# First relative bias formed behind the first slice, its tables loaded ahead of the second projection, and the front's loads put in another order

## The chip, the cores and the metric

One core of a Trainium2 chip runs the program. The metric is the device time of one execution in microseconds (us). Three runs of the kernel before took 691.38, 693.18 and 688.67 us: median 691.38.

## The reference, cut to what matters

Two layers of a decoder trunk, 256 tokens of width 1024. The change lies in the first half of layer 0, the "even mixer".

```python
cond = silu(c)
mod = cond @ ada_w[0] + ada_b[0]            # six vectors of 1024: shift, scale, gate (mixer), shift, scale, gate (ffn)
h = rmsnorm(x, mix_pre_g[0]) * (1 + scale_m) + shift_m
proj = h @ w_in                             # 1024 x 3072: qa, ka, va, qb, kb, vb, 512 columns each
# 8 heads in group a, 8 in group b, 64 wide; every head:
logit = q k^T / 8 + rel_bias[head, bucket(t - s)]      # causal
o = softmax(logit) v
y = concat(o_a, o_b) @ w_out
x = x + gate_m * rmsnorm(y, mix_post_g[0])
# then a gated feed-forward with a causal convolution of width 3, and layer 1
```

With 256 tokens group a's single block and group b's first window both become dense causal softmax attention with a bias that depends on the distance of two tokens alone; the kernel adds what the further windows of group b weigh through a table (k_reach).

## The kernel before, in words

Products of f32 are made of three matmuls each (mm3): a weight is split by ScalarE into a rounded upper part (..h, L315) and by VectorE into the remainder (..l, L316); the activations are likewise hh and hl. Engines: TensorE (PE) multiplies, VectorE (DVE) and ScalarE (ACT) split, form h, and do the softmax; SyncE (SP) issues the weight loads.

Order of work. On PE, DVE and ACT a scheduler chooses the order from the program's dependencies. SP's order is the program's own up to `in_order.close()`, and from there the scheduler places SP's DMAs too. SP has eight semaphores for its DMAs, so each waits for the one eight before it; a DMA into a buffer also waits until the buffer is free. Tiles of tag aw (a quarter of an ada_w slab, `first_ws`) have four buffers, raw weights four.

The front:
- x and c are loaded; `ada_first_load` (from L240) brings the columns of ada_w for two k-tiles as four tiles (aw_first), two DMAs each; vec_a holds ada_b and the norms' gains, turned to vT by one transposition.
- `ada_first(i)` (L220 to L238) forms shift and scale for the two k-tiles of slice i: 16 matmuls with the weights moving (`ada_main`, L154), a copy to part (L228), four transpositions (L232), three small DVE steps (L235 to L238). For slice 0, idle matmuls (`keep_clock`) stand before it and between copy and transpositions.
- `SLICES` cuts the 1024 rows of w_in into four slices of two k-tiles. Slice i loads rawaqk (two DMAs, L794) and rawav (L308), then the next slice's aw_first; turns x (xTm, L358); forms hh (L367), hsm on ACT (L371) and hl (L373); calls `ada_first(i + 1)`; and multiplies psa_q, psa_k (L813) and psa_v (L323 to L325), which add up over the slices.

Behind the fourth slice the relative bias is formed: rel_bias transposed (ps_rb, L825), multiplied with a one-hot matrix (ps_bias, L829), k_reach added (L830), and written to DRAM 32 times over (bias_d, L832, 16 x 32 x 384 f32, 786 KB). The loads of conv vectors (vec_b, L845 to L848) follow. `bias_tables` (from L854) then reads bias_d back, shifted by one element per row, into bt tiles: eight DMAs of 131 KB for the eight heads of a group. `attend` adds bt to the scores while it takes the row maximum (ltab, L582), exponentiates, transposes and multiplies with v. `qkv_proj` forms psb (L477) and psb_v for group b from rawb and rawbv; `out_proj` forms y0m (L692). `more_ada` spreads further columns of ada_w (aw_2048 and on, L143) over these parts; one kind sums on DVE (acc, L199), another on PE (L154).

## Time and profile before

| what | us |
|---|---|
| median of three runs | 691.38 |
| their range | 688.67 to 693.18 |
| the profiled execution | 693.11 |
| its span (first to last instruction) | 690.4 |
| busy: PE / DVE / ACT | 668.0 / 525.3 / 369.7 |
| mean granted clock of TensorE | 0.993 |

The profile is of one execution, 1.73 us above the median, with 2.71 us outside its span. PE's busy time is modelled for pipelined matmuls, so a busy PE is not PE at its peak: the issue cadence of matmuls (0.12 us for 256 columns, 0.23 us for 512) says what the work itself needs. A number in square brackets behind a timeline's row is the idle time before it and what ended it.

### The profile page before, as it was taken

Reading aid. Unit: us, or ns where it says so; the run is one execution under the profiler, and the core shown is the slowest. Engines: PE = TensorE matmul, PEld = TensorE weight load, DVE = VectorE, ACT = ScalarE, POOL = GpSimd, SP = SyncE. Lnnn points to the kernel's source line nnn. Section 1 sums busy time; section 2 is a strip of 40 time slices with the busy share of each in tenths; the row PEclk is TensorE's granted clock in tenths of the full one; section 3 lists DMA queues with packets and bytes.
Section 4 is the critical chain, followed back from the end, with each engine's and each line's share of the span. In section 5 each row is a group of like instructions: output and inputs, shape, how many; then the busy total and the mean of one; then the engine's idle time right before and its main releaser. Section 6 shows DMA issues by size and latency. Waiting matters only on the chain.

```text
span 690.4 us, 11784 instructions
## 1 busy us (share of the span) xinstructions
PE 668.0 (97%) x4547; PEld 574.7 (83%) x4547; DVE 525.3 (76%) x1008; ACT 369.7 (54%) x645; POOL 32.8 (5%) x95
## 2 busy tenths in 40 slices
PE   7889999999999999999999999999999999999996
PEld 5777976476899999999986998767599999999995
DVE  1454558688899999999978787774788777777785
ACT  3433455655565555555655645864565555555552
POOL 2000000001000000000001002410200000000000
PEclk9899999999999999999999999999999999999999
DMA  7799998996858878888875867622267555555611
GB/s 249 261 321 388 294 290 287 299 373 237 293 191 299 268 257 302 264 257 277 281 275 184 289 219 272 212 75 92 80 188 231 193 183 183 183 184 186 188 53 61
DMA packets 100819, 159.11 MB, mean 230 GB/s; under 512 B 4088, under 2 KB 62612, under 8 KB 100764
## 3 DMA queue, kind: packets, MB, share of 16 engines
q1 hardware_dynamic: 100739, 158.35, 68.9%
q8 instruction: 35, 0.57, 0.3%
q14 instruction: 21, 0.16, 0.1%
q10 hardware_dynamic: 24, 0.02, 0.0%
HBM read 156.52 MB, written 1.84 MB: 229 GB/s over the span
## 4 chain that ended last, share of the span: by engine, by line
PE 82%; DMA 7%; DVE 4%; ACT 2%; issue 1%; POOL 1%; SPq 1%; DVEq 0%; POOLq 0%; ACTq 0%
PE u L477 36%; PE y1f L692 9%; PE y0f L692 9%; PE psd L477 3%; DMA aw_first<-in_ada_w 3%; PE y1m L692 2%; DMA bias_d<-bias 2%; PE y0m L692 2%; DMA aw<-in_ada_w 1%; DMA bt<-bias_d 1%; PE ada L154 1%; PE psa_q L813 1%; PE psa_k L813 1%; PE ada_first L154 1%; ACT junknm L335 1%
## 5 line engine op out<-in xcount | busy, mean ns | idle before, releaser
L741 ACT ACTIVATE cv<-u,cvT 128x256 f32<-128x256 f32 x88 | 49.2, 561 | 65.6 <-PE u L477 61.7
L477 PE MATMUL u<-hh,wu_0h 128*128 128x256 f32 x352 | 69.9, 280 | 1.2 <-DVE hh L431 1.2
L477 PE MATMUL u<-hh,wu_1h 128*128 128x256 f32 x352 | 70.1, 280 | 0.0
L477 PE MATMUL u<-hh,wu_1l 128*128 128x256 f32 x352 | 69.9, 279 | 0.0
L477 PE MATMUL u<-hh,wu_0l 128*128 128x256 f32 x352 | 69.5, 279 | 0.0
L315 ACT CAST wu_1h<-rawu 128x1024 fp32r<-128x1024 f32 x44 | 46.3, 1051 | 31.1 <-PE y1f L692 17.6
L742 DVE SCALAR_TENSOR_TENSOR cv<-u,cvT,cv 128x255 f32<-128x255 f32 x88 | 42.1, 478 | 26.9 <-ACT cv L741 26.8
L199 DVE SCALAR_TENSOR_TENSOR acc<-aw,cpad,acc 128x512 f32<-128x512 f32 x77 | 57.8, 751 | 0.9 <-DMA aw<-in_ada_w 0.4
L477 PEld LDWEIGHTS u<-hh,wu_0h 128*128 128x128 f32 x352 | 54.7, 188 | 4.2 <-PE ada L276 1.4
L316 DVE TENSOR_TENSOR wu_0l<-rawu,wu_0h 128x1024 fp32r<-128x1024 f32 x44 | 53.6, 1221 | 5.3 <-ACT wu_0h L315 5.3
L315 ACT CAST wu_0h<-rawu 128x1024 fp32r<-128x1024 f32 x44 | 46.0, 1046 | 18.9 <-PE u L477 18.9
L316 DVE TENSOR_TENSOR wu_1l<-rawu,wu_1h 128x1024 fp32r<-128x1024 f32 x44 | 53.6, 1219 | 3.0 <-ACT wu_1h L315 2.9
L477 PEld LDWEIGHTS u<-hh,wu_1l 128*128 128x128 f32 x352 | 53.7, 188 | 0.0
L477 PEld LDWEIGHTS u<-hh,wu_1h 128*128 128x128 f32 x352 | 53.7, 188 | 0.0
L477 PEld LDWEIGHTS u<-hh,wu_0l 128*128 128x128 f32 x352 | 53.5, 188 | 0.0
L477 PE MATMUL u<-hl,wu_1h 128*128 128x256 f32 x352 | 48.2, 279 | 0.0
L477 PE MATMUL u<-hl,wu_0h 128*128 128x256 f32 x352 | 48.2, 279 | 0.0
L315 ACT CAST wd_0h<-rawd 128x1024 fp32r<-128x1024 f32 x26 | 27.3, 1049 | 35.3 <-PE u L477 29.9
L477 PEld LDWEIGHTS u<-hl,wu_1h 128*128 128x128 f32 x352 | 44.2, 188 | 0.0
L477 PEld LDWEIGHTS u<-hl,wu_0h 128*128 128x128 f32 x352 | 44.2, 188 | 0.0
L744 DVE SCALAR_TENSOR_TENSOR cv<-u,cvT,cv 128x254 f32<-128x254 f32 x88 | 41.8, 478 | 1.4
L316 DVE TENSOR_TENSOR wd_0l<-rawd,wd_0h 128x1024 fp32r<-128x1024 f32 x26 | 31.8, 1222 | 13.6 <-ACT wd_0h L315 13.5
(556 smaller groups left out, 1561.3 us busy)
## 6 DMA issues: line engine op xcount, KB each, us to landing
rawu<-in_ffn_w_up SPq DMA_DIRECT2D x44, 1024.0 KB, 5.5
aw<-in_ada_w SPq DMA_DIRECT2D x80, 512.0 KB, 6.6
rawd<-in_ffn_w_down SPq DMA_DIRECT2D x22, 1024.0 KB, 4.9
aw_first<-in_ada_w SPq DMA_DIRECT2D x32, 256.0 KB, 5.9
rawaqk<-in_ab_w_in SPq DMA_DIRECT2D x8, 512.0 KB, 6.5
rawb<-in_ab_w_in SPq DMA_DIRECT2D x4, 1024.0 KB, 13.9
rawd<-in_cd_w_in SPq DMA_DIRECT2D x4, 1024.0 KB, 5.8
rawc<-in_cd_w_in SPq DMA_DIRECT2D x4, 544.0 KB
```

Of the source, the lines that this page charges most:

```text
L154: last_main[:] = [nc.tensor.matmul(ps[32 * j:32 * j + 32, 0:cols], cpad[:, k, :], ws[k // 2][:, k % 2, 0:cols], start=(n < 4), stop=(n >= ...
L199: nc.vector.scalar_tensor_tensor(acc, w, c_k, acc, op0=ALU.mult, op1=ALU.add)
L315: nc.scalar.copy(hi, src)
L316: low = nc.vector.tensor_tensor(lo, src, hi.bitcast(F32), op=ALU.subtract)
L335: nc.scalar.activation(junk, src, AF.Square, scale=D ** -0.5, accum_out=ss)
L477: nc.tensor.matmul(dst(f), w[:, k, f * P:(f + 1) * P], h[:, 4 * u + k, :], start=(u == 0 and first(f) and f not in seen), stop=(u == 1 and ...
L692: last_down[:] = [nc.tensor.matmul(ys[t][:, h, :], g[p // 2][:, t * P:(t + 1) * P], wu[p % 2][:, h * 512:(h + 1) * 512], start=start and p ...
L741: nc.scalar.activation(tt[:, s, :], u_ps, AF.Identity, bias=cvT[:, bcol:bcol + 1], scale=col(2))
L742: nc.vector.scalar_tensor_tensor(tt[:, s, 1:S], u_ps[:, 0:S - 1], col(1), tt[:, s, 1:S], op0=ALU.mult, op1=ALU.add)
L744: nc.vector.scalar_tensor_tensor(tt[:, s, 2:S], u_ps[:, 0:S - 2], col(0), tt[:, s, 2:S], op0=ALU.mult, op1=ALU.add)
L813: nc.tensor.matmul((pq, pk)[f // 4][:, f % 4 // 2, f % 2 * S:(f % 2 + 1) * S], w[:, f * P:(f + 1) * P], h[:, kk, :], start=(kk == 0 and f ...
```

## The change

- The first slice's aw_first loads stand in one run, ahead of vec_a; the three small loads for the bias move behind the second slice's aw_first.
- `ada_first` becomes a generator that pauses behind its copy, so that vT is turned behind slice 0's `ada_main`, not ahead of it. Slice 0's copy moves from ACT to DVE, and its idle matmuls between copy and transpositions go from six calls to three.
- The bias is formed behind slice 0's products; bias_d is written from slice 1's place in SP's order, ahead of rawaqk of slice 2.
- Group a's eight bt loads stand in slice 3's place, behind its rawav. So they are ahead of rawb, the weights of group b's projection.
- The conv vectors are loaded and turned behind that projection, in the part whose order the scheduler chooses; SP's fixed order now ends ahead of `attend`.

```diff
--- before.py
+++ after.py
@@ -107,8 +107,8 @@
 
     vec_c = const.tile([8, P], F32, name="vec_c")
     nc.sync.dma_start(vec_c, c.rearrange("b (k p) -> (b k) p", p=P))
-    def turned(src, n, name):
-        ps = bank(f"ps_{name}", "a")
+    def turned(src, n, name, tag="a"):
+        ps = bank(f"ps_{name}", tag)
         nc.tensor.transpose(ps[:, :n], src[:n, :], ident[:n, :n])
         dst = const.tile([P, n], F32, name=name)
         nc.vector.tensor_copy(dst, ps[:, :n])
@@ -225,9 +225,10 @@
             keep_clock(before)
         ps, part = bank(f"ada_first{i}", "a"), small(f"part_first{i}", tag="part")
         ada_main(ps, first_ws[i], cols, i > 0)
-        nc.scalar.copy(part[:, 0:cols], ps[:, 0:cols])
+        (nc.scalar.copy if i else nc.vector.tensor_copy)(part[:, 0:cols], ps[:, 0:cols])
         if behind:
             keep_clock(behind, last_main[0])
+        yield
         for b in range(2 * n):
             nc.tensor.transpose(ps[:, b * P:(b + 1) * P], part[:, b * P:(b + 1) * P], ident)
         k = slice(k0, k0 + n)
@@ -769,23 +770,28 @@
         xns.append(normed(t, ss, f"m0_{t}"))
     first_mods = const.tile([P, 2, KT], F32, name="first_mods")
     B, A = first_mods[:, 0, :], first_mods[:, 1, :]
-    first_ws = {0: [ada_first_load(0, u) for u in range(2)]}
+    first_ws = {0: [ada_first_load(0, u) for u in range(4)]}
     vec_a = small("vec_a", (P, P), tag="o")
     nc.sync.dma_start(vec_a[0:96, :], ada_b.rearrange("l (k p) -> (l k) p", p=P))
     nc.sync.dma_start(vec_a[96:112, :], mix_pre_g.rearrange("l (k p) -> (l k) p", p=P))
     nc.sync.dma_start(vec_a[112:128, :], ffn_pre_g.rearrange("l (k p) -> (l k) p", p=P))
-    rb = small("rb", (16, 32), tag="o")
-    oh = small("oh", (32, TW), tag="o")
-    bias = small("bias", (16, TW), tag="o")
-    for dst, src in ((rb, rel_bias), (oh, k_onehot), (bias, k_reach)):
-        nc.sync.dma_start(dst, src)
-    first_ws[0] += [ada_first_load(0, u) for u in range(2, 4)]
-    vT = turned(vec_a, P, "vT")
-    ada_first(0, 9, 6)
+    first = ada_first(0, 9, 3)
+    next(first)
+    vT = turned(vec_a, P, "vT", "g")
+    list(first)
     w_in = ab_w_in[0]
     qkv = qkv_tiles("a")
     pq, pk = y_tile("psa_q"), y_tile("psa_k")
     pv = [bank(f"psa_v{t}") for t in range(2)]
+    def bias_tables(h0):
+
+        t = qkv_tile(f"bt{h0}")
+        for i in range(4):
+            nc.sync.dma_start(t[32 * i:32 * i + 32], bass.AP(
+                tensor=bias_d.tensor, offset=bias_d.offset + h0 * 32 * TW + P - 1 - 32 * i,
+                ap=[[TW - 1, 32], [32 * TW, 4], [1, S]]))
+        return t
+
 
     for i, (k0, n) in enumerate(SLICES):
         w = w_in[k0 * P:(k0 + n) * P]
@@ -795,6 +801,17 @@
         raw_v = load(w[:, 1024:1536], n, 512, f"rawav_{i}")
         if i + 1 < len(SLICES):
             first_ws[i + 1] = [ada_first_load(i + 1, u) for u in range(4)]
+        if i == 0:
+            rb = small("rb", (16, 32), tag="o")
+            oh = small("oh", (32, TW), tag="o")
+            bias = small("bias", (16, TW), tag="o")
+            for dst, src in ((rb, rel_bias), (oh, k_onehot), (bias, k_reach)):
+                nc.sync.dma_start(dst, src)
+        if i == 1:
+            bias_d = dram.tile([16, 32, TW], F32, name="bias_d")
+            nc.sync.dma_start(bias_d, bias[:, None, :].to_broadcast([16, 32, TW]))
+        if i == 3:
+            tabs_a = [bias_tables(4 * g) for g in range(2)]
         xb = bank(f"xTm0_{i}")
         ks = list(range(k0, k0 + n))
         xT = {k: xb[:, (k - k0) * S:(k - k0 + 1) * S] for k in ks}
@@ -802,7 +819,7 @@
             turn(xT, t, ks, xns[t])
         h_part(xT, ks, slice(0, S), A, B, f"m0_{i}")
         if i + 1 < len(SLICES):
-            ada_first(i + 1)
+            list(ada_first(i + 1))
         for k in range(n):
             kk = k0 + k
             with tc.issue_after(last_h[0].ins) if i == 0 else nullcontext():
@@ -820,21 +837,31 @@
             for t in range(2):
                 tt = (slice(None), kk, slice(t * P, (t + 1) * P))
                 mm3(pv[t], (hh[tt], hl[tt]), (wu[0][:, k, :], wu[1][:, k, :]), start=(kk == 0), stop=(kk == KT - 1))
-
-    ps = bank("ps_rb", "a")
-    nc.tensor.transpose(ps[0:32, 0:16], rb, ident[0:16, 0:16])
-    rbT = const.tile([32, 16], F32, name="rbT")
-    nc.vector.tensor_copy(rbT, ps[0:32, 0:16])
-    ps = bank("ps_bias", "a")
-    nc.tensor.matmul(ps[0:16, 0:TW], rbT, oh, start=True, stop=True)
-    nc.vector.tensor_add(bias, ps[0:16, 0:TW], bias)
-    bias_d = dram.tile([16, 32, TW], F32, name="bias_d")
-    nc.sync.dma_start(bias_d, bias[:, None, :].to_broadcast([16, 32, TW]))
+        if i:
+            continue
+
+        ps = bank("ps_rb", "a")
+        nc.tensor.transpose(ps[0:32, 0:16], rb, ident[0:16, 0:16])
+        rbT = const.tile([32, 16], F32, name="rbT")
+        nc.vector.tensor_copy(rbT, ps[0:32, 0:16])
+        ps = bank("ps_bias", "a")
+        nc.tensor.matmul(ps[0:16, 0:TW], rbT, oh, start=True, stop=True)
+        nc.vector.tensor_add(bias, ps[0:16, 0:TW], bias)
     for half in range(2):
         keep_feat(qkv[0], HD ** -0.5)(half, pq[:, half, :])
         keep_feat(qkv[1])(half, pk[:, half, :])
     keep_v(qkv[2], pv)
 
+    in_order.close()
+
+    def pairs_ab(group, q, k, v):
+        tabs = [bias_tables(group * 8 + 4 * i) for i in range(2)] if group else tabs_a
+        return [SoftmaxPair(head_rows(q, p), head_rows(k, p), head_values(v, p),
+                            [tabs[p // 2][:, 2 * (p % 2) + j, :] for j in range(2)],
+                            f"ab{group}_{p}", group * 4 + p, group * 4 + p in (1, 4, 6)) for p in range(4)]
+
+    gs = attend(pairs_ab(0, *qkv), "a")
+    qkv = qkv_proj(w_in, 1536, "b")
 
     cvT = const.tile([P, 352], F32, name="cvT")
     cw = ffn_conv_w.rearrange("l j (k p) -> (l j k) p", p=P)
@@ -849,25 +876,6 @@
         ps = bank(f"ps_cv{i}", "a")
         nc.tensor.transpose(ps[:, :n], v[:n, :], ident[:n, :n])
         nc.vector.tensor_copy(cvT[:, i * P:i * P + n], ps[:, :n])
-    in_order.close()
-
-    def bias_tables(h0):
-
-        t = qkv_tile(f"bt{h0}")
-        for i in range(4):
-            nc.sync.dma_start(t[32 * i:32 * i + 32], bass.AP(
-                tensor=bias_d.tensor, offset=bias_d.offset + h0 * 32 * TW + P - 1 - 32 * i,
-                ap=[[TW - 1, 32], [32 * TW, 4], [1, S]]))
-        return t
-
-    def pairs_ab(group, q, k, v):
-        tabs = [bias_tables(group * 8 + 4 * i) for i in range(2)]
-        return [SoftmaxPair(head_rows(q, p), head_rows(k, p), head_values(v, p),
-                            [tabs[p // 2][:, 2 * (p % 2) + j, :] for j in range(2)],
-                            f"ab{group}_{p}", group * 4 + p, group * 4 + p in (1, 4, 6)) for p in range(4)]
-
-    gs = attend(pairs_ab(0, *qkv), "a")
-    qkv = qkv_proj(w_in, 1536, "b")
     gs += attend(pairs_ab(1, *qkv), "b")
     ys = y_tiles("y0m")
     out_proj(ys, ab_w_out[0], gs[0:4], True, False, "o0a")
```

On SP before, from slice 3's loads on (names end in the tile's number; bias_d stands last):

```order
L794 DMA rawaqk_575<-in_ab_w_in 128x1024 x2
L308 DMA rawav_578<-in_ab_w_in 128x2x512
L308 DMA rawb_0_973<-in_ab_w_in 128x4x512
L308 DMA rawb_1_1031<-in_ab_w_in 128x4x512
L143 DMA aw_2048_0_765<-in_ada_w 128x2x512
L143 DMA aw_2048_1_767<-in_ada_w 128x2x512
L143 DMA aw_2048_2_769<-in_ada_w 128x2x512
L143 DMA aw_2048_3_771<-in_ada_w 128x2x512
L256 DMA gate_2_773<-in_mix_post_g 128x1024
L308 DMA rawb_0_1093<-in_ab_w_in 128x4x512
L308 DMA rawb_1_1151<-in_ab_w_in 128x4x512
L832 DMA bias_d<-bias 512x1x384
```

After, around bias_d in its new place, behind slice 2's aw_first:

```order
L245 DMA aw_first_0_342<-in_ada_w 128x2x256 x2
L245 DMA aw_first_1_345<-in_ada_w 128x2x256 x2
L245 DMA aw_first_2_348<-in_ada_w 128x2x256 x2
L245 DMA aw_first_3_351<-in_ada_w 128x2x256 x2
L812 DMA bias_d<-bias 512x1x384
L800 DMA rawaqk_460<-in_ab_w_in 128x1024 x2
L309 DMA rawav_463<-in_ab_w_in 128x2x512
```

And after, from slice 3's loads on:

```order
L800 DMA rawaqk_581<-in_ab_w_in 128x1024 x2
L309 DMA rawav_584<-in_ab_w_in 128x2x512
L790 DMA bt_586<-bias_d 32x4x256 x4
L790 DMA bt_591<-bias_d 32x4x256 x4
L309 DMA rawb_0_953<-in_ab_w_in 128x4x512
L309 DMA rawb_1_1011<-in_ab_w_in 128x4x512
L143 DMA aw_2048_0_745<-in_ada_w 128x2x512
L143 DMA aw_2048_1_747<-in_ada_w 128x2x512
L143 DMA aw_2048_2_749<-in_ada_w 128x2x512
L143 DMA aw_2048_3_751<-in_ada_w 128x2x512
```

bias_d moved from behind rawb to ahead of rawaqk of slice 2, and group a's eight bt loads now stand ahead of rawb and aw_2048.

On PE before, the end of slice 0 (ada_first_240 is the sum for slice 1):

```order
L813 MATMUL psa_k_208<-hl,waqk_1h 128x256
L154 MATMUL ada_first_240<-aw_first_3_226,cpad 32x512 x2
L154 MATMUL ada_first_240<-aw_first_2_223,cpad 32x512 x2
L154 MATMUL ada_first_240<-aw_first_1_220,cpad 32x512 x2
L154 MATMUL ada_first_240<-aw_first_0_217,cpad 32x512 x2
L813 MATMUL psa_k_208<-hl,waqk_1h 128x256
L813 MATMUL psa_k_209<-hl,waqk_1h 128x256 x2
L324 MATMUL psa_v_210<-wav_0l,hh 128x512
```

After, the same place:

```order
L325 MATMUL psa_v_202<-wav_0l,hh 128x512
L326 MATMUL psa_v_202<-wav_0h,hl 128x512
L154 MATMUL ada_first_237<-aw_first_3_217,cpad 32x512 x2
L154 MATMUL ada_first_237<-aw_first_2_214,cpad 32x512 x2
L154 MATMUL ada_first_237<-aw_first_1_211,cpad 32x512 x2
L154 MATMUL ada_first_237<-aw_first_0_208,cpad 32x512 x2
L233 MATMUL ada_first_237<-ident,part_first_238 128x128 x4
L844 MATMUL ps_rb<-ident,rb 32x16
L848 MATMUL ps_bias<-oh,rbT 16x384
L830 MATMUL psa_q_197<-hh,waqk_2h 128x256
```

The sum for slice 1 moved from inside psa_k to behind the last psa_v of slice 0, and the bias's two PE instructions now stand between its transpositions and slice 1's first product.

On ACT before, around slice 3's hsm (wb_0_0h is the upper part of group b's first weights):

```order
L315 CAST waqk_7h<-rawaqk_575 128x1024
L315 CAST wav_3h<-rawav_578 128x1024
L371 ACTIVATE hsm_3_585<-xTm_3_580,first_mods 128x256 x2
L315 CAST wb_0_0h<-rawb_0_973 128x1024
L315 CAST wb_1_0h<-rawb_0_973 128x1024
```

After:

```order
L228 COPY part_first_489<-ada_first_488 128x512
L316 CAST wav_3h<-rawav_584 128x1024
L316 CAST wb_0_0h<-rawb_0_953 128x1024
L372 ACTIVATE hsm_3_601<-xTm_3_596,first_mods 128x256 x2
L316 CAST wb_1_0h<-rawb_0_953 128x1024
```

The cast of rawb_0 moved ahead of slice 3's hsm; on DVE wb_0_0l likewise moved ahead of slice 3's hl, which needs that hsm.

## Rows read from the trace of the kernel before

**Rows 1.** Windows by stage: length, busy us (and instructions) per engine, clock, DMA share, GB/s.

```profile
22.40:71.70 49.30, 46.24 (x316) 37.18 (x316) 26.00 (x38) 19.78 (x27) 0.00 (x0) 0.97 0.91 323
71.70:93.00 21.30, 21.30 (x181) 20.47 (x181) 10.60 (x21) 7.16 (x10) 0.00 (x0) 1.00 0.91 241
93.00:168.40 75.40, 73.81 (x406) 49.48 (x404) 59.49 (x168) 44.63 (x117) 1.73 (x4) 1.00 0.95 324
```

**Rows 2.** Timeline of TensorE in the front: start us, us, instruction, idle before and releaser.

```profile
16.64 1.05 PE L154 MATMUL ada_first<-aw_first,cpad 128*32 128x512 f32 x4 [2.44 <-DMA aw_first<-in_ada_w]
17.63 2.56 PE L124 MATMUL idle<-ones 128*128 128x128 f32 x12
...
22.44 0.48 PE L813 MATMUL psa_q<-hh,waqk_0h 128*128 128x256 f32 x2 [1.40 <-DVE hh L367]
```

**Rows 3.** Finer windows, same columns as rows 1.

```profile
2.00:8.00 6.00, 6.00 (x43) 5.86 (x43) 1.12 (x5) 1.91 (x7) 1.61 (x5) 1.00 0.95 322
...
9.00:11.00 2.00, 1.71 (x15) 1.36 (x13) 0.38 (x1) 0.92 (x3) 0.87 (x2) 1.00 0.29 78
...
29.00:33.00 4.00, 4.00 (x38) 2.71 (x36) 2.28 (x2) 1.05 (x1) 0.00 (x0) 1.00 0.04 14
...
45.00:66.00 21.00, 21.00 (x150) 16.95 (x149) 12.66 (x21) 8.81 (x12) 0.00 (x0) 1.00 1.02 362
...
74.00:80.00 6.00, 6.00 (x53) 5.54 (x52) 2.10 (x2) 1.05 (x1) 0.00 (x0) 1.00 0.87 164
...
88.00:92.00 4.00, 4.00 (x36) 4.00 (x36) 0.72 (x4) 0.04 (x1) 0.00 (x0) 1.00 0.61 123
```

**Rows 4.** Chain of waits, start us, us, what; first projection to the first softmax, then y0m.

```profile
31.50 1.85 PE ada_first L154 x16
...
36.02 6.33 DMA aw_first<-in_ada_w
...
53.96 1.85 PE ada_first L154 x16
...
63.33 0.93 PE psa_k L813 x8
...
66.55 13.62 DMA bias_d<-bias
...
81.88 9.50 DMA bt<-bias_d
...
91.62 0.29 DVE ltab L582
...
152.20 2.78 PE y0m L692 x12
```

**Rows 5.** Groups of TensorE instructions, 71.7 to 168.4 us: count, busy us, mean ns.

```profile
L596 PE MATMUL sab<-ident,ltab 128*128 128x128 f32 x48 | 8.2, 278 | 0.0
...
L477 PE MATMUL psb<-hh,wb_1h 128*128 128x256 f32 x32 | 7.1, 298 | 0.0
```

**Rows 6.** Timeline of SyncE's DMA issues: start us, us of issuing, count.

```profile
9.40 2.14 SPq L244 DMA_DIRECT2D aw_first<-in_ada_w  x4
...
59.37 3.90 SPq L308 DMA_DIRECT2D rawb<-in_ab_w_in  x2
...
80.18 10.26 SPq L858 DMA_DIRECT2D bt<-bias_d  x8
```

**Rows 7.** One tile, rawb: ns min/median/max, first and last start us; issue to landing.

```profile
L308 SPq DMA_DIRECT2D rawb<-in_ab_w_in x4: 643/900/1129, 50.3 to 62.6; - x4
...
DMA to landing us min/median/max: 13.9/13.9/13.9
```

**Rows 8.** Timeline of ScalarE at slice 3's hsm, columns as rows 2.

```profile
61.25 1.01 ACT L371 ACTIVATE hsm<-xTm,first_mods 128x256 f32<-128x256 f32 x2
62.16 1.05 ACT L315 CAST wb_0h<-rawb 128x1024 fp32r<-128x1024 f32 x1
```

**Rows 9.** Timeline of VectorE at slice 3's hl, columns as rows 2.

```profile
62.61 0.67 DVE L373 TENSOR_TENSOR hl<-hsm,hh 128x512 fp32r<-128x512 f32 x1
```

## The prediction

> **What bounds the kernel now.** I cut the span at the places where the work changes hands and read the windows [rows 1]. From 22.4 to 71.7 us (group a's projection) PE is busy for 46.2 of 49.3 us with DMA at 0.91; from 71.7 to 168.4 us (group b's projection, attention, y0m) PE shows no gap worth naming, with DMA at 0.91 and 0.95. PE and DMA both run nearly full up to 168 us, and a transfer that is moved mostly pushes another. The order of PE from the first u on is the same in both kernels, so whatever the change does is decided before that, and all behind it only shifts.
>
> The second view was PE's timeline of the front [rows 2]: the reader sees PE wait 2.44 us for the last aw_first tile at 16.64 us, then 2.56 us of idle matmuls, and the first product at 22.44 us. The third was finer windows [rows 3], which show where DMA has holes: 78 GB/s from 9 to 11 us, 14 GB/s from 29 to 33 us, against 362 GB/s from 45 to 66. The fourth was the chain of waits [rows 4]: the second hole ends because ada_first for slice 1 (31.50 us, 1.85 us long) frees the aw buffers; bias_d then takes 13.62 us to land and bt 9.50 us, and the first softmax step starts at 91.62 us, 20 us behind the scores' operands.
>
> Busy PE hides waits there. Its own work from 71.7 to 168.4 us, by cadence: psa_k shows 8 matmuls of 256 columns in 0.93 us, 0.117 each; y0m 12 of 512 columns in 2.78 us, 0.232 each [rows 4]. There are six psb groups of 32 like the one of [rows 5] (22.5 us), six psb_v groups of 8 (11.1 us), 96 y0m matmuls, eight pieces like the one of 12 (22.3 us), and 176 small matmuls of the softmax pairs (48 transpositions [rows 5] and four kinds of 32) at about 0.11, near psa_k's cadence, 19.4 us. With three ada sums of 1.85 us (5.6) and about 3 us of gate and mod rows that is 84 us of 96.7. Some 13 us are stalls that the page counts as busy; I call that an estimate, good to 3 us.
>
> **Part by part.**
>
> *Front.* In the record the second half of slice 0's aw_first is issued only at 9.40 us [rows 6], behind six small loads. In one run, x, the four tiles and vec_a are 3.1 MB from about 2 us on, at 322 to 362 GB/s [rows 3] 8.6 to 9.6 us: the last tile lands at 10.6 to 11.6, I take 11.4, against 16.64. The sum itself then costs 1.05 us as before. Three idle calls fewer of six take half of the 2.56 us, 1.2 us. First psa_q: 22.44 - 5.2 - 1.2 = 16.0, so -6.4 us. vT, now turned behind the sum, hides behind the copy; x's transpositions, moved there too, do the same. Bounds: -4 (the weights of slice 0, 1.5 MB behind 3.1 MB, land late, at 4.6 MB / 0.322 + 2 = 16.3, and their splits are 2.3 us) to -7.5.
>
> *Slice 0 to slice 1.* ada_first for slice 1 stood 9.06 us behind the first psa_q [rows 2, 4]; now three psa_k (0.12 each) and ten psa_v (0.232) come first, 2.7 us. It starts at 16.0 + 11.8 = 27.8 against 31.50: -3.7. What the front gains, this gives back by 2.7, since the aw buffers for slice 2 come free only behind it and SP stands still until then. The bias's two PE instructions and its copy and addition add about 1 us here; they leave the end of slice 3 (before, they also stood between products there), so I set them at 0, within 0 to +1.
>
> *bias_d.* 786 KB. From 74 to 80 us, when it is nearly alone, DMA is 0.87 busy at 164 GB/s [rows 3]: 0.98 MB in 5.2 busy us, so 4.2 us at least for bias_d; the whole window, 6 us, at most. Before, its 13.62 us [rows 4] lay beside products. Now it stands ahead of rawaqk of slice 2 and of slice 3's aw_first, where DMA is full. I take 6: slice 3's aw_first lands at -3.7 + 6 = +2.3. ada_first3 waited for nothing at 53.96 us [rows 4]; with an unseen reserve of about 1 us it goes to 55.3, and slice 3 to about +1.
>
> *bt.* From 88 to 92 us, bt nearly alone: 123 GB/s at 0.61 busy [rows 3], 0.49 MB in 2.4 busy us, so 1.05 MB take 5.2 us. This now comes ahead of rawb_0. Before, the cast of rawb_0 at 62.16 us [rows 8] had no wait, and stood behind slice 3's hsm. Now ACT and DVE both put rawb_0's split ahead of slice 3's hsm and hl. Behind hl wait 32 products of q and k (0.117 each) and nine of v (0.232), 5.8 us of PE. rawb_0's bytes come -3.7 + 6 + 5.2 = +7.5 us later than before. Its old landing is not shown. At latest, in strict order behind slice 3's aw_first (at hand by some 53 us), rawaqk and rawav (2.5 MB with its own, 6.9 us at 362 GB/s [rows 3]): 59.9. At earliest 6.3 us behind its issue at 50.3 [rows 7], the 6.33 us that an aw_first took to land [rows 4]: 56.6. So now it lands between 64.1 and 67.4. With the cast (1.05), two hsm (1.0 together [rows 8]) and hl (0.7 [rows 9]) the end of psa comes, 5.8 us later, at 72.6 to 75.9, against 71.7: +0.9 to +4.2. I take the middle, +2.6, that is 74.3.
>
> A rule of the Trainium skill ("DMA: Bandwidth & Descriptors", section "Queues, rings and completion order") speaks against this middle: DMAs of one issuing engine share one ring on each of the 16 DMA engines, which is consumed in order. By it rawb_0 starts only when all of bt has started, so the upper end holds, +4.2, and the sum below would be -0.3. The trace agrees in part: a rawb took 13.9 us to land [rows 7], with slabs ahead of it that SP had issued before 59.4 [rows 6].
>
> *Behind the projection.* Before, bt's eight issues took SP 10.26 us from 80.18 on [rows 6], and landed at 91.4. Now bt is there when the scores are, so group a's softmax (DVE, ACT) can run beside all of psb instead of from 91.6 us on. DVE is busy for 10.6 of 21.3 us from 71.7 to 93 and for 59.5 of 75.4 after it [rows 1]: the load becomes even. Of the 13 us of stalls I take 4.5 away. Not more, because group b's softmax, which was filled with psb_v, now has only y0m beside it, and DMA at 0.95 from 93 us on brings the aw and rawo0c tiles no sooner. Bounds: -12 (nearly all stalls gone) to +4 (new waits of 2 us at group a's start and 2 at group b's).
>
> *Conv vectors.* Their four loads and transpositions leave 67 to 94 us for a place beside psb; they are needed only in the feed-forward. Cost 0, cover: DVE's free half. If that cover goes, 1 us.
>
> *Clock.* From 22.4 to 71.7 us the granted clock is 0.97 [rows 1], so all that its dips can give back is 0.03 x 49.3 = 1.5 us. A front in which PE idles less may have fewer of them. I count 0.
>
> **Sum.** +2.6 at the end of group a's projection, -4.5 behind it: -1.9. The profiled execution took 693.1, so 691.2; it lay 1.7 above the median of the runs, so 689.5 us.
>
> **The rivals.**
> 1. *rawb_0 holds group a (slower).* The wait for bt is replaced by one for rawb_0: ACT and DVE, in order, hold slice 3's hsm and hl behind its split. Each microsecond that it lands behind 63.1 moves T0, the end of psa, by one; it decides from a landing at 68 us, when bias_d and bt cost more than 12 us together or rawb_0 before landed near 60: T0 = 68 + 2.8 + 5.8 = 76.6, +5. The slabs of ada_2048, which stand behind rawb, then come no earlier than group a's scores, so that nothing is gained there: 691.4 + 5 = 696.4. For it: DMA full from 45 to 66 us [rows 3]. Against it: the front's 3.7 us are already counted in.
> 2. *The bias fits beside (faster).* bias_d and bt are slow only when alone, because few bytes are in flight; among other transfers they take 1.8 MB / 0.362 = 5 us in place of 11, spread over holes that are left (14 GB/s in a window of 4 us [rows 3]). Then T0 keeps the front's -3.7, and -4.5 comes on top: 691.4 - 8.2 = 683.2. For it: all of DMA's holes before 45 us. Against it: its busy share of 0.87 at 164 GB/s, which says that bias_d occupies the engines and not only the clock.
> 3. *The early softmax buys nothing.* PE shows no gap from 71.7 to 93 [rows 1], and if its cadence there is what its operands allow, the stalls stay: +2.6 alone, 691.4 + 2.6 = 694.0.
>
> **How the numbers follow.** Forecast 0.40, rival 1 0.17, rival 2 0.25, rival 3 0.18. A measurement of this kernel tells about 1%, 6.9 us, from no change: 684.5 and 698.3. Rival 2 and the fast end of the forecast (stalls -9) lie below: 0.26. Only rival 1 with a second wait (group b's start, +4) lies above: 0.12. Range: from rival 2 with the clock's 1.5 us, 681.5, to rival 1 with half of that price, 698. The forecast's own range is 685 to 694.
>
> **What would show it.** Right: first psa_q near 16 us; ada_first for slice 1 near 28 and slice 2's aw_first issued behind it; psa ending 73 to 76 us with hl of slice 3 behind wb_0_0l; first ltab near psa's end; first u near 175. Wrong: psa ending before 70 us (rival 2), or a PE gap before the last psa_q or at ada_2048 of over 3 us (rival 1). The whole falls if the first psa_q isn't earlier at all, since then the reordered run of loads is bound by something that I did not see.

## The result and the profile after

The changed kernel took 711.50 us (median of 4 runs, 710.67 to 716.24); the kernel before, run beside it, 690.02 (4 runs). The ratio is 1.0323, 95% interval 1.028 to 1.0366. The prediction, 689.5 within 681.5 to 698, was wrong.

The profiled execution took 710.67 us, 17.6 more than that of before. A second profile of the kernel before, taken later (e12 below, 688.41 us), is the better measure: the first one had a slow clock in its front, as shown below. All "against before" from here on is against this second profile. The table has start times in us on TensorE, from one profile of each kernel. T0 is the start of the last psa matmul (the end of group a's projection), "ka" group a's first scores, "kb" group b's, y0m the output projection, u the first product of the feed-forward:

| kernel | first psa_q, slice 0 / 2 / 3 | T0 | ka | kb | first y0m | first u | ka to u |
|---|---|---|---|---|---|---|---|
| before, first profile | 22.44 / 50.57 / 62.12 | 71.34 | 71.67 | 119.82 | 138.04 | 176.83 | 105.2 |
| before, second (e12) | 21.61 / 47.55 / 59.10 | 68.32 | 68.65 | 115.94 | 134.49 | 173.12 | 104.5 |
| after | 17.35 / 51.82 / 64.93 | 76.31 | 77.63 | 138.93 | 157.28 | 195.27 | 117.6 |

At the first u the change is 22.15 us behind, and the medians differ by 21.5: all is lost before the first u, 8.0 of it by T0, 1.0 to ka and 13.2 behind ka. Against the first profile, from which the prediction was worked out, it is 18.4: 5.0 by T0 and 13.5 behind it.

The windows of after (columns as in [rows 1]); the first three rows answer to [rows 1], the next three to [rows 3], and the last two cut the third in half:

```profile
17.35:77.63 60.28, 48.93 (x324) 37.32 (x324) 26.52 (x39) 20.90 (x29) 0.00 (x0) 0.94 0.96 293
77.63:138.93 61.30, 61.30 (x380) 43.28 (x376) 37.82 (x92) 28.22 (x63) 0.00 (x0) 1.00 0.78 272
138.93:157.28 18.35, 10.70 (x56) 6.52 (x55) 14.77 (x53) 10.39 (x32) 0.00 (x0) 0.65 1.04 305
...
28.00:33.00 5.00, 2.71 (x22) 0.77 (x12) 3.31 (x8) 1.83 (x3) 0.00 (x0) 0.89 0.59 193
...
39.00:45.00 6.00, 5.53 (x46) 3.72 (x44) 0.00 (x0) 0.00 (x0) 0.00 (x0) 1.00 0.93 167
45.00:66.00 21.00, 16.03 (x112) 12.78 (x113) 10.72 (x17) 8.29 (x10) 0.00 (x0) 1.00 1.01 306
139.00:148.40 9.40, 5.06 (x36) 3.39 (x35) 5.96 (x11) 3.42 (x4) 0.00 (x0) 0.79 1.04 262
148.40:157.30 8.90, 5.59 (x20) 3.08 (x20) 8.74 (x42) 6.99 (x28) 0.00 (x0) 0.50 1.03 350
```

PE is now idle for 11.4 us of group a's projection (before 2.6), and for 7.7 us ahead of y0m (before 0.8). From 39 to 45 us DMA is 0.93 busy at 167 GB/s and neither DVE nor ACT has anything to do: this is where bias_d is written.

The same stretches of before's second profile, and its front:

```profile
17.00:28.00 11.00, 8.63 (x64) 7.28 (x65) 5.50 (x9) 4.46 (x6) 0.00 (x0) 1.00 1.05 365
21.61:68.65 47.04, 44.43 (x316) 35.26 (x316) 25.86 (x38) 19.72 (x27) 0.00 (x0) 1.00 0.99 352
68.65:115.94 47.29, 47.29 (x330) 39.05 (x329) 32.96 (x80) 25.14 (x56) 0.00 (x0) 1.00 0.90 290
115.94:134.49 18.55, 17.80 (x109) 8.40 (x108) 11.83 (x49) 12.81 (x36) 0.00 (x0) 1.00 0.99 295
...
28.00:33.00 5.00, 5.00 (x37) 3.11 (x36) 1.92 (x2) 2.82 (x4) 0.00 (x0) 1.00 0.73 257
```

And the first profile of before, in the same two stretches of the front:

```profile
17.00:28.00 11.00, 8.82 (x44) 7.32 (x41) 5.50 (x9) 4.69 (x7) 0.00 (x0) 0.70 1.06 370
28.00:33.00 5.00, 5.00 (x45) 3.71 (x43) 2.45 (x2) 1.85 (x2) 0.00 (x0) 0.97 0.15 58
```

The first execution ran its front at a granted clock of 0.70 on average, a mixture of the two levels (1.2 and 2.4 GHz); the second at 1.00. The sum for slice 1 began at 31.43 in the first and at 28.99 in the second, and the DMA hole of [rows 3] is that of the first: from 28 to 33 us DMA moved 58 GB/s in the first and 257 in the second.

TensorE's timeline of the front of after, answering to [rows 2]:

```profile
13.12 1.05 PE L154 MATMUL ada_first<-aw_first,cpad 128*32 128x512 f32 x4 [0.62 <-DMA aw_first<-in_ada_w]
14.10 0.94 PE L124 MATMUL idle<-ones 128*128 128x128 f32 x6
...
17.35 0.48 PE L830 MATMUL psa_q<-hh,waqk_0h 128*128 128x256 f32 x2 [1.33 <-DVE hh L368]
...
27.42 1.92 PE L154 MATMUL ada_first<-aw_first,cpad 128*32 128x512 f32 x16
...
32.48 1.46 PE L848 MATMUL ps_bias<-oh,rbT 32*16 32x384 f32 x2 [1.23 <-DVE rbT L846]
```

SyncE's issues of after, answering to [rows 6] and to bias_d and bt in [rows 4]:

```profile
28.52 3.97 SPq L245 DMA_DIRECT2D aw_first<-in_ada_w  x8
34.55 0.69 SPq L812 DMA_DIRECT2D bias_d<-bias  x1
35.34 4.79 SPq L800 DMA_DIRECT2D rawaqk<-in_ab_w_in  x2
40.22 3.03 SPq L309 DMA_DIRECT2D rawav<-in_ab_w_in  x1
...
52.71 6.25 SPq L790 DMA_DIRECT2D bt<-bias_d  x7
...
130.41 4.38 SPq L143 DMA_DIRECT2D aw<-in_ada_w  x4
...
136.22 10.64 SPq L790 DMA_DIRECT2D bt<-bias_d  x8
```

SP stands from 32.5 to 34.55 us because bias_d needs the bias, which PE, DVE, PE and DVE form in turn from 31 to 34.5; the two issues of rawaqk behind it then take 4.79 us where before's second profile had 0.89.

The chain of waits of after, answering to [rows 4, 8, 9]:

```profile
44.91 7.78 DMA aw_first<-in_ada_w
...
52.71 9.28 DMA bt<-bias_d
...
62.06 5.71 DMA rawb<-in_ab_w_in
...
67.87 1.05 ACT wb_0h L316
...
70.09 0.70 DVE hl L374
...
138.92 9.29 DMA bt<-bias_d
...
148.45 0.29 DVE ltab L583
```

The waits themselves stand in the timelines of ACT, PE and DVE:

```profile
67.87 1.04 ACT L316 CAST wb_0h<-rawb 128x1024 fp32r<-128x1024 f32 x1 [5.32 <-DMA rawb<-in_ab_w_in]
70.83 0.74 PE L830 MATMUL psa_q<-hl,waqk_6h 128*128 128x256 f32 x4 [2.83 <-DVE hl L374]
...
148.45 0.29 DVE L583 CUSTOM_DVE_ANT_0 ltab<-sab,bt 128x128 f32<-128x128 f32 x1 [2.83 <-DMA bt<-bias_d]
150.98 1.12 PE L171 MATMUL ada<-ident,acc 128*128 128x128 f32 x4 [4.89 <-DVE cvT L878]
```

SP issued rawb_0 only at 62.06, when the first of bt's eight DMAs had landed, and ACT casts it at 67.87, after 5.32 us of idle time. hsm and hl stand behind that cast, and PE waits 2.83 us for hl: rival 1, to the step. Seventy microseconds later the tables of group b make a second wait: DVE's first softmax step waits for bt, and PE's longest idle time there, 4.89 us, ends with a copy (cvT) that DVE does behind these steps.

Against group b's scores these tables are no later than before. Their issue begins 2.7 us ahead of kb in after; in before's second profile, where kb is at 115.94, it begins 2.1 us ahead:

```profile
113.86 5.53 SPq L858 DMA_DIRECT2D bt<-bias_d  x5
```

Before, PE had other work there.

### The profile page after: what moved, and what is told of

Read it like the earlier page. It is cut to its first block, busy times and chain, and to the rows that moved or that the text cites. A ratio compares the mean times of both kernels' runs of the same rounds, so it can differ in the third digit from the quotient of the medians.

```text
span 708.9 us, 11770 instructions
## 1 busy us (share of the span) xinstructions
PE 674.7 (95%) x4541; PEld 575.5 (81%) x4541; DVE 527.2 (74%) x1009; ACT 370.3 (52%) x644; POOL 32.8 (5%) x95
## 3 DMA queue, kind: packets, MB, share of 16 engines
q1 hardware_dynamic: 100739, 158.35, 67.8%
## 4 chain that ended last, share of the span: by engine, by line
PE 81%; DMA 7%; DVE 4%; SPq 3%; ACT 3%; issue 1%; POOL 1%; DVEq 0%; POOLq 0%; ACTq 0%
PE u L478 35%; PE y1f L693 8%; PE y0f L693 8%; PE psb L478 3%; PE psd L478 3%; DMA bt<-bias_d 3%; PE y0m L693 2%; PE y1m L693 2%; DMA aw_first<-in_ada_w 2%; PE ada L154 2%; PE sab L605 1%; PE sab L597 1%; DMA rawb<-in_ab_w_in 1%; ACT junknm L336 1%; SPq L245 1%
## 5 line engine op out<-in xcount | busy, mean ns | idle before, releaser
L316 ACT CAST wu_1h<-rawu 128x1024 fp32r<-128x1024 f32 x44 | 46.3, 1052 | 31.1 <-PE y1f L693 17.6
L317 DVE TENSOR_TENSOR wd_0l<-rawd,wd_0h 128x1024 fp32r<-128x1024 f32 x26 | 31.8, 1224 | 13.4 <-ACT wd_0h L316 13.2
```

The lines of the kernel that those rows point to most:

```text
L316: nc.scalar.copy(hi, src)
L317: low = nc.vector.tensor_tensor(lo, src, hi.bitcast(F32), op=ALU.subtract)
```

## The experiments

Theory A at first: three transfers in new places (bias_d, group a's bt ahead of rawb_0, group b's bt late) make the loss, and the front is a gain. Theory C: the front itself costs. Each recorded text explains its own letters. What each run's profile showed:

| run | psa_q slice 2 | T0 | ka | kb | first y0m | first u | ka to u | median (ratio, 95%) |
|---|---|---|---|---|---|---|---|---|
| e1 | 49.88 | 71.46 | 71.79 | 125.19 | 140.95 | 179.09 | 107.3 | 695.70 (1.0083, 1.0042 to 1.0125) |
| e8 | 45.37 | 67.68 | 68.01 | 122.20 | 140.84 | 178.97 | 111.0 | 692.55 (1.0033, 1.0006 to 1.0059) |
| e10 | 47.45 | 69.77 | 70.10 | 123.43 | 137.30 | 177.00 | 106.9 | 691.91 (1.0034, 1.0009 to 1.0058) |
| e11 | 44.79 | 67.10 | 67.42 | 120.53 | 134.95 | 173.88 | 106.5 | 690.96 (1.0028, 1.0004 to 1.0052) |
| e13 | 47.66 | 68.44 | 68.77 | 116.82 | 137.38 | 176.04 | 107.3 | 688.87 (0.9991, 0.9966 to 1.0016) |
| e2 | 53.53 | 75.67 | 77.84 | 132.95 | 145.69 | 186.01 | 108.2 | 700.41 (1.0156, 1.0124 to 1.0188) |
| e3 | 53.25 | 74.94 | 76.26 | 136.42 | 159.07 | 197.14 | 120.9 | 712.47 (1.0327, 1.0298 to 1.0355) |
| e4 | 48.62 | 77.02 | 77.43 | 133.17 | 147.21 | 186.68 | 109.3 | 699.82 (1.0143, 1.0113 to 1.0173) |
| e5 | 53.27 | 78.85 | 80.17 | 141.47 | 154.99 | 193.44 | 113.3 | 708.95 (1.0261, 1.0214 to 1.0308) |
| e6 | 52.86 | 73.94 | 75.26 | 135.17 | 148.78 | 187.92 | 112.7 | 704.13 (1.0193, 1.0142 to 1.0244) |
| e7 | 47.36 | 73.19 | 75.36 | 133.41 | 148.29 | 187.72 | 112.4 | 703.20 (1.0171, 1.0119 to 1.0223) |
| e9 | 52.51 | 77.95 | 79.28 | 138.02 | 154.81 | 195.66 | 116.4 | 709.57 (1.0283, 1.0246 to 1.0321) |
| e14 | 53.19 | 74.51 | 75.83 | 123.50 | 148.24 | 188.90 | 113.1 | 703.86 (1.0211, 1.0167 to 1.0255) |
| e15 | 52.36 | 73.32 | 74.64 | 134.52 | 146.82 | 185.75 | 111.1 | 701.55 (1.0167, 1.0129 to 1.0205) |
| e16 | 52.14 | 73.09 | 74.42 | 125.73 | 145.74 | 185.60 | 111.2 | 700.19 (1.0147, 1.0111 to 1.0183) |
| e17 | 51.87 | 73.00 | 74.33 | 122.01 | 146.90 | 189.00 | 114.7 | 703.64 (1.0175, 1.0124 to 1.0227) |

How far a single profile can be trusted behind ka is shown by e13: its order there is that of before, and it took 107.3 where before's two profiles took 105.2 and 104.5. Differences under 3 us in that column are not read below. In front of ka profiles with the same order differ nearly as much: slice 2 starts between 44.79 and 47.45 in e8, e10 and e11, and between 51.82 and 53.53 in the ten profiles that have bias_d where after has it.

**e1, the front alone** on the kernel before (first loads in one run, the pause in `ada_first`, three idle calls):

```diff
-    first_ws = {0: [ada_first_load(0, u) for u in range(2)]}
+    first_ws = {0: [ada_first_load(0, u) for u in range(4)]}
...
-    first_ws[0] += [ada_first_load(0, u) for u in range(2, 4)]
...
-    ada_first(0, 9, 6)
+    first = ada_first(0, 9, 3)
...
```

> The kernel before with the front's part of the change alone (first slice's four aw_first tiles in one run, vT turned behind the sum, copy on VectorE, three idle calls); the bias, its tables and the conv vectors stay where they were. Theory A (the front gains, the loss comes from the bias's transfers): first psa_q at 17 to 18 us, the end of group a's projection near 68 us, 685 to 688 us. Theory C (the front itself costs): 692 us or more.

Theory C: no gain, rather a loss of 0.8%, and T0 is 3.1 us behind before. The first psa_q came at 17.29 us, but the sum for slice 1 at 28.95, as in before's second profile (28.99), and slice 2 began 2.3 us later than there. In the hole behind that sum the windows show, for e1

```profile
28.00:33.00 5.00, 3.53 (x25) 1.33 (x23) 3.05 (x5) 3.33 (x4) 0.00 (x0) 1.00 0.40 133
```

against 0.73 and 257 GB/s before: the products are done sooner, and PE and DMA are idle together until that sum frees the buffers. Why slice 2 then comes later than before, and not at the same time, isn't shown.

**e8, the front with slice 1's sum put ahead** of slice 0's second k-tile and hl products; **e13** is this edit alone on the kernel before; **e12** is the kernel before again.

```diff
+                        with tc.issue_after(last_main[0].ins) if i == 0 and (k or h is hl) else nullcontext():
...
```

> As e1_front_only, and on TensorE the sum for slice 1 (ada_first) is held ahead of slice 0's products with hl and of its second k-tile, instead of behind all of slice 0's psa_v. Theory A (the hole in DMA at 28 to 33 us, with SyncE waiting for the aw buffers that this sum frees, is what eats the front's gain): the sum at 22 to 26 us, slice 2's aw_first issued by 27 instead of 30, end of group a's projection at 68 to 70 us instead of 71.5, 688 to 692 us. Theory I (the bytes alone pace the slices): end of the projection unchanged within 1 us, 694 to 697 us.

> The kernel before, unchanged, to see how far its steps move from one profiled execution to the next. If the first profile (693.1 us) is a late one of this kernel's spread (686 to 694), the end of group a's projection or the first u come 3 to 5 us earlier here; every comparison of steps with the first profile is then good to that much only. If they agree within 1 us, the spread lies behind the first u.

> The kernel before with one edit: on TensorE the sum for slice 1 is held ahead of slice 0's products with hl and of its second k-tile (as in e8, without the change's front). Theory A (that sum frees the aw buffers, and DMA stands still from 28 to 33 us until it does): the sum at 28 to 29 us instead of 31.5, end of group a's projection 2 to 3 us earlier; as group b's tables then are later than its scores, first u at most 2 us earlier: 686 to 690 us. Theory I (the bytes alone pace the slices): the same within 1 us, 689 us.

e12 took 689.16 (ratio 1.0008, 0.9976 to 1.0039). In e8 the aw_first issues start at 27.74, not 30.04, and the hole is filled:

```profile
28.00:33.00 5.00, 5.00 (x44) 4.24 (x36) 3.86 (x5) 3.36 (x4) 0.00 (x0) 1.00 0.91 300
```

Slice 2 then starts 4.5 us earlier than in e1 and T0 falls by 3.8, but to 67.68, only 0.6 ahead of before, and the median does not go under before's. So the hole was what cost in e1 (theory A of e8; by theory I T0 would have stayed), and with it filled the front is level with before, not ahead. In e13 the edit could move the sum only from 28.99 to 28.46, and T0 and the median are those of before.

**e10 and e11, e8 with all tables asked for together** ahead of group a's attention (e11 with nine buffers for q, k, v and bt instead of eight):

```diff
-        tabs = [bias_tables(group * 8 + 4 * i) for i in range(2)]
+        tabs = tabs_ab[group]
...
```

> As e8_front_ada1, with group b's tables asked for ahead of attention a. Theory A (e8 gained 3.8 us at the end of group a's projection and lost it again because TensorE waited for group b's tables at 130 to 135 us): no such wait, first u at 172 to 175 us instead of 179.0, 685 to 689 us, that is faster than the kernel before. Theory J (behind group a's projection DMA's bytes set the end, whatever the order): first u at 177 or later, 691 us or more.

> As e10_front_ada1_tabsb, with a ninth buffer for q, k, v and tables (and twelve instead of thirteen of the small work tiles), so that group b's k and v need not wait for buffers that the early tables hold. Theory A: no slower than e10, up to 3 us faster if there TensorE waits for psb's banks; else the same within 1 us.

Medians 691.91 and 690.96: theory J for e10, and e11 within what was expected of it. No run of this study beats the kernel before.

**e7, bias_d small.** e5 (below) with bias_d written once, 25 KB for 786, and the tables' rows read reversed within each 32, so that the bias isn't the reference's.

```diff
...
-            nc.sync.dma_start(bias_d, bias[:, None, :].to_broadcast([16, 32, TW]))
+            nc.sync.dma_start(bias_d, bias)
```

> As e5_btb, with bias_d written once (16 x 384, 25 KB) instead of 32 times (786 KB); the tables are then read from it with their rows in reversed order within each 32, so the scores' bias isn't the reference's. Theory A (bias_d ahead of slice 2's weights holds DMA for 6 to 8 us): slice 2 starts at 46 to 48 us instead of 51.8, slice 3 at 58 to 61 instead of 64.9, end of group a's projection at 70 to 73 instead of 76.3. Theory H (bias_d goes beside the others and bt ahead of rawb is the whole delay): slices 2 and 3 earlier by under 1.5 us, end of the projection as in e5_btb within 1.5.

Slice 2 starts at 47.36, against 53.27 in e5: bias_d costs 5.9 us there (4.5 against after itself), and without it slice 2 stands where before had it (47.55). The gain lasts: the median is 5.7 under e5's. The window of e7 in which bias_d stood:

```profile
39.00:45.00 6.00, 6.00 (x52) 4.40 (x51) 2.59 (x3) 2.59 (x3) 0.00 (x0) 1.00 0.91 313
```

The same busy share as in after moves 313 GB/s for 167.

**e4, bias_d late:** formed early, but written behind slice 3's loads, ahead of rawb; group a's tables and the conv vectors are placed as before.

```diff
-        if i == 1:
+        if i == 3:
             bias_d = dram.tile([16, 32, TW], F32, name="bias_d")
...
```

> The changed kernel with the bias formed behind slice 0 as there, but all its transfers late: bias_d behind slice 3's loads, bt placed by the scheduler, conv vectors at their old place. Theory A: slices 2 and 3 keep the front's gain, end of group a's projection near 68 to 70 us plus what bias_d ahead of rawb costs (up to 4), 685 to 691 us. Theory D' (the bias's PE and VectorE steps between slice 0 and 1 cost): no better than e1_front_only by 2 us or more and slice 1 later by over 1 us.

Slice 2 starts at 48.62, without bias_d's price, but T0 is 77.02, as late as in after and 3 us beyond the latest that was expected (74; the median of 699.82 is 9 us above its range). rawb_0 now stands behind bias_d, and PE waits for hl as in after, only longer:

```profile
69.28 1.22 PE L828 MATMUL psa_q<-hl,waqk_6h 128*128 128x256 f32 x4 [4.01 <-DVE hl L374]
```

**e2, group a's tables back** where the scheduler puts them:

```diff
-        if i == 3:
-            tabs_a = [bias_tables(4 * g) for g in range(2)]
...
```

> The changed kernel with one edit: group a's eight bt loads go back behind the projection, where the scheduler places them, so they are no longer ahead of rawb. Theory A (bt ahead of rawb costs some 4 us at the end of group a's projection, and SyncE's order, which also put group b's bt behind aw_4608, some 10 us in attention b): end of group a's projection at 72 to 73 us, group b's bt landed before its scores, 690 to 696 us. Theory B (the early softmax beside psb is what costs): as slow only if the softmax is early; then 695 us or less too, but with bt of group b still late. Theory D (bias_d ahead of slice 2's weights is the main cost): 706 us or more.

T0 falls by 0.6 only, not by the 3 to 4 us expected, and the median of 700.41 lies between the theories' ranges. Slices 2 and 3 began 1.7 and 1.3 us later in this profile; from slice 3's first product to T0 it took 9.5 us (before 9.2) against 11.4 in after and 12.2 to 12.9 in e5, e7 and e9, which have the same order there, so bt ahead of rawb_0 costs 1.9 to 3.4 there. But from ka to u it takes 9.4 us less than after. So the greater part of the loss behind ka comes with the early tables, where I had expected a gain.

**e3, the conv vectors back** in their old place:

> The changed kernel with one edit: the conv vectors' loads and transpositions go back to their old place ahead of the second projection. Theory A: slice 3's hl is no longer behind rawb_0's split (the order shows it), so the end of group a's projection comes 1 to 3 us earlier, but group b's bt is still issued behind aw_4608 and the wait in attention b stays: 706 to 711 us. Theory E (the moved conv vectors are what made group b's bt late): 696 to 700 us.

No difference in the median (1.0327 for 1.0323). hl now comes ahead of rawb_0's split, PE no longer waits for it, and from slice 3 to T0 it takes 8.4 us in place of 11.4. So e3 removes rival 1's wait too, by the scheduler's order (e4, with the same place for the conv vectors, keeps it). T0 is 1.4 us better, but PE's wait for group b's softmax, 7.7 us in four pieces in after, is now one of 12.29:

```profile
152.38 0.95 PE L597 MATMUL sab<-ident,ltab 128*128 128x128 f32 x3 [12.29 <-DVE ltab L594]
```

**e5, group b's tables ahead of the loads of aw_4608** on SP's queue, and **e6, in addition the split of rawb_0 held behind slice 3's hsm and hl:**

```diff
+            with tc.issue_after(last_bt[0].ins) if (layer, c0) == (0, 4608) else nullcontext():
...
+            with tc.issue_after(last_hs[0].ins), tc.issue_after(last_hl[0].ins):
                 wu = split(raw[:, :, half * 256:(half + 1) * 256], [P, 4, 256], f"w{name}_{half}_{u}")
```

> The changed kernel with one edit: on SyncE the four loads of aw_4608 stand behind group b's eight bt loads instead of ahead of them. Theory A (group b's tables are late because aw_4608, which waits for buffers until its turn on TensorE, is queued ahead of them): bt issued at 125 to 127 us instead of 136, landed by 136, TensorE's idle stretch of 9 us at group b's softmax gone with its cold clock; first u at 185 to 187 us instead of 195.3; 700 to 703 us. Theory F (the tables are slow because DMA is full there): issued earlier but landed at 145 or later, 708 us or more.

> As e5_btb, and besides the split of rawb_0 is held behind slice 3's hsm on ScalarE and hl on VectorE. Theory A: the 2.8 us that TensorE waits for hl go, end of group a's projection at 73 to 74 us instead of 76.3; then rawb is what group b's projection waits for, so half of it or less stays: 698 to 702 us. Theory G (the order of those two on ScalarE and VectorE is the cause of the late end): all 2.8 us stay to the end, 697 to 700 us.

e5 missed what was expected, bt issued at 125 to 127 us and a median of 700 to 703: another load on SP (rawu) stood ahead of bt and waited 7.5 us for its buffer, and the issue began at 136.40, 5.1 us ahead of kb (after 2.7):

```profile
136.40 6.19 SPq L792 DMA_DIRECT2D bt<-bias_d  x8
```

The eight issues take 6.19 us in place of 10.64, and ka to u falls by 4.4; e6 and e7, with the same order, have 112.7 and 112.4. So these late tables are worth about 4 to 5 us. The median falls by 2.5, as e5's T0 is 2.5 later than after's, for which no cause is shown. e6: PE no longer waits for hl (it starts at 68.57, after 70.83), T0 is 73.94, 4.9 less than in e5 and 2.4 less than in after, and the median goes down by 4.8 against e5. Rival 1's wait is real and is removed so: from slice 3 to T0 it takes 8.3 us, as in e14 to e17, and less than before. What stays of T0, 5.6 us, lies ahead of slice 3. bias_d's price is of this size; but e1, without bias_d there, is 3.1 us late as well, so the parts don't simply add, and no run leaves out bias_d's price and that wait together. The median was expected at 697 to 702 and is above that.

**e9, after with group b's tables asked for ahead of group a's attention** (issued at 74.97):

```diff
-        tabs = [bias_tables(group * 8 + 4 * i) for i in range(2)] if group else tabs_a
+        tabs = tabs_b if group else tabs_a
...
```

> The changed kernel with one edit: group b's two tables are asked for in the program ahead of attention a, not ahead of attention b, so SyncE loads them beside group b's projection, well ahead of aw_2560, aw_3072 and aw_4608. Theory A (of the 18 us lost up to the first u some 5 come by the end of group a's projection and the rest by group b's tables being late): tables b landed before 110 us, no wait over 1.5 us for them, first u at 183 to 186 us instead of 195.3, 700 to 702 us. Theory B (the early softmax beside psb costs by itself): end of psb_v as late as in the changed kernel (138 us) and first u at 189 or later, 704 us or more.

Theory B: nothing gained. The chain of e9 has no bt any more ahead of y0m, but in its place

```profile
136.14 4.00 DMA aw<-in_ada_w
...
149.28 8.66 DMA aw<-in_ada_w
```

**Is it the cover?** A new theory: before, half of group a's softmax stood beside group b's scores and covered group b's own softmax; the change moved it away (PE has 109 instructions between kb and y0m before, 56 after). e14 is e6 with group a's later pairs put behind group b's projection; e15 is e6 with the tables asked for early and into buffers of their own; e16 is e15 with e14's order; e17 is e16 with the tables later.

```diff
-    gs = attend(pairs_ab(0, *qkv), "a")
+    gs = []
+    rest_a = attend_steps(pairs_ab(0, *qkv), gs, "a")
+    for _ in range(3):
+        next(rest_a)
     qkv = qkv_proj(w_in, 1536, "b")
+    list(rest_a)
```

> The sixth run's kernel (group b's tables first on their queue, the split of rawb_0 held behind slice 3's hl), with one thing more: the program gives group a's steps in two parts, the first three ahead of group b's projection and the rest behind it, so that the softmax of group a's later pairs stands beside group b's scores again. Theory A (the early softmax of group a has taken the cover of group b's): T0 stays within 1 us of the sixth run's 73.94, and from group a's scores to the first u it takes 107 to 110 us in place of 112.7; first u at 182 to 185, median 698 to 701. Theory B (the cover does not matter; what is lost behind the scores is the wait for group b's tables and the projections' own switches): from scores to first u 112 us or more, median 703 or above. Between them, 110 to 112: part of it, left open.

> The sixth run's kernel with group b's tables asked for ahead of group a's attention, into buffers of their own (ten buffers of tag qkv for eight, 11 of t for 13, 7 of o for 8). No wait for these tables is left; group a's softmax is as early as in the change. Theory A (the cover of group b's softmax is what is missing): from group a's scores to the first u 111 us or more, against 112.7 in the sixth run. Theory B (only the late tables and the wait for aw behind them): 108 us or less.

> The run before this one, with group a's later pairs given behind group b's projection, as in the fourteenth. There group b's second table tile waited for a buffer that group a's late pairs held, so the tables landed only near 142 us and the cover could not be read; here they have buffers of their own. Theory A (cover is what is missing, once the tables are there): from group a's scores to the first u at least 3 us less than in the run before this one, 106 to 109; first u 181 to 184, median 697 to 700. Theory B (cover does not matter): within 1.5 us of the run before this one.

> The sixteenth run's kernel with group b's tables asked for later: behind the loads of aw_4608, rawo0c and the first rawu, ahead of aw_2560, some 4 us ahead of group b's scores, as they stand in the sixth run; still in buffers of their own, still with group a's later pairs behind group b's projection. In the sixteenth run the tables stood ahead of the second rawbv and of aw_4096, and TensorE stood idle for 2 us of 84 to 94 us and ran slowly around it. Theory A (tables in time and a cover for group b's softmax together are all that is missing): from group a's scores to the first u 105 to 108 us, first u at 179 to 182, median 694 to 697. Theory B (something else: where the transfers stand on a full queue decides, and cover is worth little): 110 us or more, median 699 or above.

The cover came back (106 PE instructions between kb and y0m in e14 and e17, 114 in e16), and nothing was gained: 113.1 against e6's 112.7, 111.2 against e15's 111.1, 114.7. By the bounds on record theory A fails in e14, e16 and e17; e15 alone, at 111.1, met its bound of 111. The cleanest pair is e16 against e15, which differ in the cover alone; in e14 the last of the tables was issued only at 131.22, 7.7 us behind kb. In each of them another transfer on SP's queue stands in the chain. The chain of e17, ahead of the first sum behind kb:

```profile
117.62 5.95 DMA bt<-bias_d
123.59 5.16 DMA aw<-in_ada_w
...
128.88 1.05 PE ada L157 x4
```

and ACT of e16, in group b's projection, with the tables early:

```profile
89.22 1.04 ACT L319 CAST wb_0h<-rawb 128x1024 fp32r<-128x1024 f32 x1 [5.97 <-DMA bt<-bias_d]
```

In e13, too, where the order is that of before, this is what its slower stretch shows:

```profile
114.31 9.09 DMA rawu<-in_ffn_w_up
123.46 6.89 DMA aw<-in_ada_w
```

Such a row alone doesn't explain the loss, since the chain of before's second profile has one too, with PE busy for 17.80 of the 18.55 us between kb and y0m:

```profile
121.53 5.93 DMA aw<-in_ada_w
```

**What stays open.** Of the 13.2 us behind ka, e2 gives 9.4 back, and e5 shows about 4 of these as the late tables. How the rest comes about isn't settled. The cover is not it. Where it lies can be estimated, by counting every matmul of the timelines at the cadence of its kind (0.117 us for 256 columns, 0.232 for 512, 0.11 for the small ones, 0.116 in an ada sum). Between ka and kb PE takes some 11 us more than that in after, 8 in e2 and 2 in before's second profile; between kb and y0m some 12, 5 and 5. A few records are missing, so each figure is good to about 2 us. So the wait that can be seen ahead of y0m is about half of the loss, and most of what e2 gives back; the other half lies in group b's projection, where PE shows no idle time (61.30 of 61.30 us) and no single piece is over 0.75 us. An order that keeps the early tables of group a and has no load late wasn't found.

## Why the prediction was wrong, point by point

- *Front, -6.4.* Right in kind, too large: psa_q at 17.35 (forecast 16.0), -5.1 against [rows 2] and -4.3 against the second profile; the last tile let PE start at 13.12, not 11.4. "First psa_q isn't earlier", on which the whole was to fall, didn't happen.
- *Slice 0 to slice 1, -3.7.* The sum came at 27.42 (forecast 27.8), yet the step failed. The 31.50 it was taken from, and the hole of [rows 3], belonged to one execution with its front at a clock of 0.70; against 28.99 the gain is 1.6. And e1 shows that what the front gains is gone by slice 2: it starts 2.3 us later than before. Both sums rested on PE's times, where bytes and buffers set the pace (DMA at 1.05 from 17 to 28 us).
- *Clock, 0 to 1.5.* The wrong step behind that: I priced the dips by the mean, 0.03 x 49.3, and only from 22.4 us on. The second profile's first u is 3.7 us earlier than the first's, 3.0 of it already at T0; the stretch with the dip (0.70 from 17 to 28 us) began before my window, and it delayed a sum for which SP and DMA stood still.
- *bias_d, 6.* Right in size: 5.9 in e7 against e5, 4.5 against after. The reserve of 1 us was right to be small: slice 3 came at 64.93, 5.8 behind the second profile, where I had +1, since the front's 3.7 were not there to be set against it.
- *bt and rawb_0, +2.6 at T0.* The mechanism was right, and the stronger bound held: rawb_0 landed at 67.8, beyond the 67.4 of the upper end. The rule of the Trainium skill that I had set beside it ("DMA: Bandwidth & Descriptors", section "Queues, rings and completion order": one issuer's DMAs share rings that are consumed in order) isn't tested by this: SP issued rawb_0 only at 62.06, when the first bt, eight DMAs ahead of it, had landed, so the order was SP's already. Rival 1 put the end of psa at 76.6 for a landing at 68; measured 76.7 for 67.8 (T0 is the start of its last matmul, 76.31). I gave it 0.17. But e2 corrects its share: bt ahead of rawb_0 costs 1.9 to 3.4 us, and most of T0's 8.0 is that the slices before it were late already. What helps against the rest is to hold the split (e6).
- *Behind the projection, -4.5.* This step failed most: +13.2, or +12.4 from ka on against the first profile. The stalls that I wanted to take away, 13 us of PE's time over its matmuls' cadence, are about 12 in before's second profile by the same sum (96 us from ka to the last y0m, less 84). They are not one wait, but spread thin, in part at switches between kinds of matmul. In the second profile's timeline,

```profile
112.61 0.65 PE L604 MATMUL sab<-ptsab,va 128*64 128x256 f32 x2
113.19 0.50 PE L324 MATMUL psb_v<-wbv_1l,hh 128*128 128x512 f32 x1
113.53 0.40 PE L325 MATMUL psb_v<-wbv_1h,hl 128*128 128x512 f32 x1
113.76 0.39 PE L323 MATMUL psb_v<-wbv_1h,hh 128*128 128x512 f32 x1
```

  one psb_v follows the next after 0.23 us, but the one behind the softmax's matmuls takes 0.34, and those two 0.58. An earlier softmax doesn't take such switches away, and no run with it got any of the 12 us back. My upper bound, two new waits of 2 us, was too small: PE is idle for 7.7 us ahead of y0m, where a bt of group b landed 9.29 us behind its issue, with DMA at 1.04 (9.50 for group a's before, [rows 4], but there beside products), and by the estimate above PE's time in group b's projection rose by about as much again, for which the cause stays open. I named DMA "at 0.95" as a reason for a smaller gain and asked neither what stands late on SP if eight loads change their place nor what PE is left to do while it waits.
- *Conv vectors, 0.* Right for the median within what e3 can tell; T0 is 1.4 us better there, as hl comes ahead of rawb_0's split.
- *Rival 2* (the bias fits beside) is refuted by e7, *rival 3* (the early softmax buys nothing) was right that nothing is gained there, but had no loss in it.
